# An encoder layer on one core: which engine copies the first up pair's sums, and in what order its second pieces and the LN1 columns run

## The chip, the cores and the metric

The kernel runs on one core of a Trainium2 chip. The metric is the device time of one execution in microseconds (us). TensorE (PE in the profile) does the matrix products, VectorE (DVE), ScalarE (ACT) and GpSimd (POOL) the elementwise work, and SyncE (SP) issues most DMAs. PSUM is the memory that matrix products are written to. Every engine has a queue of its own, and semaphores hold an instruction until what it needs is there.

## The reference, cut to what matters

Two batches, 512 and 256 tokens of 1024 channels, go through one layer with shared weights. `u` is 2 x 2816 wide; the change lies where the first LayerNorm of the layer passes over into the product `x @ w_up`.

```
x = layernorm(x)                                         # ln_in
proj = x @ w_in                                          # 1024 -> 3072
y = concat(rmsnorm(conv mixer), rmsnorm(2-D neighbourhood attention))
x = layernorm(ALPHA * x + y @ w_o, ln1_g, ln1_b)         # LN1
u = dwconv3(x @ w_up, ffn_conv_w, ffn_conv_b)            # 1024 -> 2 * 2816
gate, val = split(u)
x = layernorm(ALPHA * x + (gelu(gate) * val) @ w_down)   # 2816 -> 1024
```

## The kernel before, in words

The 768 tokens are kept as six tiles of 128 (`acc[t]`), tiles 0, 2, 4 of even tokens and 1, 3, 5 of odd ones. All operands are split in a high and a low fp32r part (`split`, lines 98 to 100: ScalarE casts the high part, VectorE or GpSimd subtracts for the low one), and a product is three fp32r products.

**The way into the up projection.** `wo_conv(t)` (lines 815 to 827) ends the mixer's output projection of a tile and normalises it: VectorE adds the product to `acc[t]` (L823), sums up (L824, L209), ScalarE squares (L210), VectorE and GpSimd make the inverse root (L211, L212), VectorE the offset (L826), and ScalarE applies both (L827). `x_tr(t)` (lines 833 to 845) transposes the tile on TensorE (L250) in two halves of four blocks of 128 and applies LN1's gain and offset by column while it takes them out of PSUM: eight instructions a tile, on ScalarE (L844) or, for the second half of odd tiles, on VectorE (L842). `x_even(a)` and `x_odd(a)` (lines 852 to 870) split the columns and make the sums that the products want (L862 to L869), which land in the tile `AR`, seven operands with 386 columns each; columns 0 to 255 come from tiles 0 to 3, columns 257 to 384 from tiles 4 and 5.

**An up pair.** 22 channel blocks of `gate` and of `val` are done pair by pair, c = 0 to 21. A pair takes seven products instead of eight (a Strassen-like scheme for even and odd tokens, gate and value), called by number: `step(c, i)` (lines 951 to 989) with i = 1, 7, 6, 2, 4, 5, 3. One product is 12 matmuls of 386 columns (L180). Four PSUM banks take the sums, called roles 1 to 4: product 1 is written to role 1, which is copied to role 2 (L957); product 7 to role 4, copied to an SBUF tile `M7` (L963); product 6 is added to role 2, which is copied to role 3 (L966); product 2 is added to role 1, product 4 to role 2, products 5 and 3 to role 3. So product 2 may be added to role 1 only once role 1 is copied, and product 4 to role 2 only once that is copied. These copies are ScalarE's before the change. Weights of a product are made by `prep` (a ScalarE cast and a VectorE subtraction of 512 columns), up to three products ahead.

**The first pair.** For c = 0, products 1, 7, 6, 2 and 4 are done in two pieces: columns 0 to 255 as soon as tiles 0 to 3 are there (`a1 a7 a6 a2 a4` in the list of line 999), and columns 256 to 385 in the later loop (the second pieces), as those need tiles 4 and 5. In the list, `w5` is `wo_conv(5)`, `e2` is `x_even(2)` (tile 4) and `o2` is `x_odd(2)` (tile 5).

**What sets the order.** In the stretch of line 999 the order on every engine but SyncE is made by the scheduler of the language, which starts from the order of the code and moves instructions past each other; from line 1125 on TensorE keeps the order of `seq` (line 1007), while the other engines are still ordered by the scheduler. Each engine then works its queue from the front.

Of the kernel before, what the change touches and what calls it, by code (L numbers as in the profile page):

```python
# [48 lines left out]
def encoder_kernel(ctx, tc, x, lnp, wv, wproj, wo_a, wo_c, wup, wdn, chan, rpb, mask, ident, out):  # L49
    nc = tc.nc  # L50
    V, A, G, PE, SP = nc.vector, nc.scalar, nc.gpsimd, nc.tensor, nc.sync
    PS = bass.MemoryType.PSUM

    def pool(name, **kw):
        g = tc.tile_pool(name=name, bufs=1, reuse_waits="tile", **kw)
        p = g.__enter__()
        return p, lambda: g.__exit__(None, None, None)
# [11 lines left out]
    def f(ap):  # L69
        return ap.bitcast(F32)  # L70
# [112 lines left out]
    a1, a1_close = pool("a1", side="right")  # L183
# [62 lines left out]
    def transposed(q, src):  # L246

        q = q.rearrange("p (k n) -> p k n", k=4)
        for k in range(4):
            PE.transpose(q[:, k], src[:, k], idt)  # L250
        return q
# [73 lines left out]
    for z in "w0 w1 w2 w3 w4 w5 x1 w6 x2 w7 x3 c0 x4 x5".split():  # L325
        n = int(z[1])
# [72 lines left out]
    a2, a2_close = pool("a2", side="right")  # L399
# [140 lines left out]
    R, M7, K = {}, {}, {}  # L540
# [208 lines left out]
    def bank(name):  # L749
        return ps.tile([P, 512], F32, name=name, tag="bank", bufs=8)  # L750
# [39 lines left out]
    for n in range(2):  # L790
        order = (4, 5, 0, 1, 2, 3)
        banks = {t: bank("wo") for t in order}
        for kk in range(2):
# [3 lines left out]
            for k in range(2):  # L797
                i = 2 * kk + k
# [13 lines left out]
    def kn(z):  # L812
        return z.rearrange("p (k n) -> p k n", n=P)
# [19 lines left out]
    def x_tr(t):  # L833

        z = []
        for c in range(2):
            q = transposed(bank("tr"), kn(acc[t])[:, 4 * c:4 * c + 4])
            z.append(lp.tile([P, 4, P], F32, name="zt", bufs=7))
            for k in range(4):
                i = 4 * c + k  # L840
                if c and t % 2:
                    V.tensor_scalar(z[c][:, k], q[:, k], g1[:, i:i + 1], b1[:, i:i + 1], op0=OP.mult, op1=OP.add)  # L842
                else:
                    A.activation(z[c][:, k], q[:, k], AF.Identity, bias=b1[:, i:i + 1], scale=g1[:, i:i + 1])  # L844
        return z
# [6 lines left out]
    def x_even(a):  # L852
        xq[a] = x_tr(2 * a)
        for c in range(2):
            x_op(xq[a][c], c, a)

    def x_odd(a):
        el, eh = xq.pop(a)
        ol, oh = x_tr(2 * a + 1)
        x_op(oh, 2, a)  # L860
        es = engs(TE[4 * a:4 * a + 4])
        V.tensor_sub(el, el, ol)  # L862
        x_op(el, 3, a, es[0])
        V.tensor_sub(ol, oh, ol)
        x_op(ol, 5, a, es[1])
        z = lp.tile([P, 4, P], F32, name="zt", bufs=7)
        V.scalar_tensor_tensor(z, el, -1.0, oh, op0=OP.mult, op1=OP.subtract)
        x_op(z, 4, a, es[2])
        V.scalar_tensor_tensor(eh, z, -1.0, eh, op0=OP.mult, op1=OP.subtract)  # L869
        x_op(eh, 6, a, es[3])  # L870
# [18 lines left out]
    def taps_even(c, u, w, b):  # L889

        A.activation(c[:, 0], u, AF.Identity, bias=b, scale=w[:, 1:2])
        A.activation(c[:, 1], u, AF.Identity, bias=b, scale=w[:, 0:1])  # L892
        tap(c, 1, u, 1, w[:, 2:3])

    def taps_odd(c, u, w):
        tap(c, 1, u, 0, w[:, 1:2])
        tap(c, 0, u, 0, w[:, 2:3])
        tap(c, 0, u, -1, w[:, 0:1])

    def cut():  # L900
        return fp.tile([P, 2, HT], F32, name="cu", bufs=6)
# [9 lines left out]
    def gated(c):  # L911

        g, v = ct.pop(c)
        V.tensor_mul(g, g, v)  # L914
        j = c // 2
        if c % 2 == 0:
            h_out(j, 0, 1, g[:, 0:1])
            ho[j] = g
            return
        o = ho.pop(j)  # L920
        h_out(j, 1, 2, g)
        z = fp.tile([P, 3, HT], F32, name="ho", bufs=1)
        V.tensor_sub(z[:, 0], g[:, 1], o[:, 1])
        V.tensor_sub(o[:, 1], o[:, 0], o[:, 1])
        h_out(j, 3, 1, o[:, 1:2])
        V.scalar_tensor_tensor(z[:, 1], o[:, 1], -1.0, g[:, 1], op0=OP.mult, op1=OP.subtract)
        V.scalar_tensor_tensor(z[:, 2], z[:, 1], -1.0, g[:, 0], op0=OP.mult, op1=OP.subtract)
        h_out(j, 4, 3, z)

    pairs, R, M7 = {}, {}, {}  # L930
# [7 lines left out]
    def role(c, i):  # L938
        if (c, i) not in R:
            R[c, i] = bank("u")[:, 0:HT]  # L940
            if i in (2, 3) and c < 2:
                w = pairs[c].w[1 if i == 2 else 6][:, 0]
                PE.matmul(R[c, i], w[:, 0:P], w[:, 0:HT], start=True, stop=True, skip_group_check=True)
        return R[c, i]

    def rest(q, n):

        if n.stop < HT:
            V.memset(q[:, n.stop:HT], 0.0)

    def step(c, i, n=slice(0, HT)):

        k = pairs[c]
        if i == 1:
            k.prod(1, role(c, 1)[:, n], n.start == 0, False, n)
            rest(role(c, 1), n)
            A.copy(role(c, 2)[:, n], role(c, 1)[:, n])  # L957
        elif i == 7:
            k.prod(7, role(c, 4)[:, n], n.start == 0, True, n)
            rest(role(c, 4), n)  # L960
            if c not in M7:
                M7[c] = fp.tile([P, HT], F32, name="m7", bufs=2) if c else M70()
            A.copy(M7[c][:, n], role(c, 4)[:, n])  # L963
        elif i == 6:
            k.prod(6, role(c, 2)[:, n], False, False, n)
            A.copy(role(c, 3)[:, n], role(c, 2)[:, n])  # L966
        elif i == 2:
            k.prod(2, role(c, 1)[:, n], False, True, n)
            if n.stop == HT:
                ct[c] = [cut(), None]  # L970
                taps_even(ct[c][0], role(c, 1), fw[:, c], fb[:, c:c + 1])
        elif i == 4:
            k.prod(4, role(c, 2)[:, n], False, True, n)
            if n.stop == HT:
                k.v = cut()
                V.tensor_add(k.v[:, 0], role(c, 2), M7[c])
        elif i == 5:
            k.prod(5, role(c, 3), False, False)
            v = ct[c][1] = cut()
            V.tensor_add(k.v[:, 1], role(c, 3), M7[c])  # L980
            taps_even(v, k.v[:, 0], fwn[:, c], fb[:, NC + c:NC + c + 1])
            taps_odd(v, k.v[:, 1], fwn[:, c])
        else:
            k.prod(3, role(c, 3), False, True)
            g = ct[c][0]
            taps_odd(g, role(c, 3), fw[:, c])
            A.activation(g, g, AF.Gelu_apprx_tanh)
            gated(c)
            pairs.pop(c)

    def M70():
        return ring.tile([P, 512], F32, name="raw", bufs=NRAW)[:, 0:HT]

    PIECE = {z: n for z in (1, 7, 6, 2, 4) for n in (slice(Z0, HT),)}
    EM = {"w": wo_conv, "e": x_even, "o": x_odd, "l": load_up,
          "p": lambda i: pairs[0].prep(i), "a": lambda i: step(0, i, slice(0, Z0))}
    V.memset(f(AR[:, :, :, :, Z0:Z0 + 1]), 0.0)
    V.memset(f(AR[:, :, :, :, Z1:Z1 + 1]), 0.0)
    for z in "l0 l1 w0 p1 w1 e0 w2 o0 p7 w3 e1 p6 w4 o1 p2 w5 e2 p4 a1 a7 o2 a6 a2 a4 p5".split():
        EM[z[0]](int(z[1]))  # L1000
    lp_close()
    bp_close()
# [3 lines left out]

    seq = []
    for c in range(NC):
        z = [(c, i) for i in (1, 7, 6, 2, 4, 5)]
        if c:  # L1010
            z.insert(2, (c - 1, 3))
        seq += z
    ready = {(0, i) for i in (1, 7, 6, 2, 4, 5)}

    def prepare(c, i):
# [109 lines left out]
    with tc.manual_schedule(engines={PE.engine}):  # L1125
        for n, (c, i) in enumerate(seq):
            if i == 7 and 0 < c < NC - 1:
                load_up(c + 1)
            step(c, i, PIECE[i] if c == 0 and i in PIECE else slice(0, HT))
            for z in seq[n + 1:n + 1 + AHEAD]:  # L1130
                prepare(*z)
            if i == 7:
                sw_slot(len(SEQB) + c)
            if c == NC - 1 and i == 1:
                load(NE)
            if c == NC - 1 and i in (6, 4):
                prep(done[1] + 1)
# [3 lines left out]
        prep(3)  # L1141
        prepare(NC - 1, 3)
        step(NC - 1, 3)
        prep(4)
        fp_close()
# [96 lines left out]
```

## Time and profile before

| | us |
|---|---|
| median of 3 runs | 865.4 |
| the three runs | 865.4, 857.47, 865.75 |
| the profiled execution, own time | 857.87 |
| its span, first to last instruction | 856.1 |

The profile is of one execution; own time and span differ by 1.8 us. In its rows, TensorE is PE, its weight loads PEld; L180 is line 180 of the kernel. A timeline row gives start, duration, engine, line, operation, output<-input, shape, count and, in square brackets, how long the engine was idle before it and what it was waiting for. Equal instructions that follow each other without idle time are one row with a count. The granted clock of TensorE stands in the window rows as PEclk, 1.00 for 2.4 GHz and 0.50 for 1.2 GHz.

### The profile page before, as it was taken

To read this page: it belongs to the slowest core of one execution; us is meant where nothing else is said; L and a number is where in the kernel's file an instruction comes from. 1 tells how busy PE (TensorE), PEld (TensorE's weight loads), DVE (VectorE), ACT (ScalarE), POOL (GpSimd) and SP (SyncE) were. 2 spreads that over 40 slices of the span, in tenths; PEclk is the share of its full clock that TensorE was granted. 3 is DMA by queue.
4 is the path that set the end of the run, shared out by engine and by line. 5 is a ranking of instruction groups with operands and counts; after the bars stand their busy time and mean duration, and the time that the engine had idled before them with its cause. 6 is when DMAs were issued, how large, how long until landed. Compare 5 with 4: busy or idle time off the path is not lost.

```text
span 856.1 us, 13322 instructions
## 1 busy us (share of the span) xinstructions
PE 814.3 (95%) x4391; PEld 750.1 (88%) x4391; DVE 684.7 (80%) x1335; ACT 494.1 (58%) x1020; POOL 231.3 (27%) x286
## 2 busy tenths in 40 slices
PE   4899999999999999899999999999999999999995
PEld 3678998989898777899999999999999968888884
DVE  6997757877876658788889888888989679995675
ACT  4755655665776448765656565555656357565060
POOL 3565361263402521222333243332211000000102
PEclk9999999999999999899999999999999999999998
DMA  8688868866836740496998998899752199894361
GB/s 323 214 211 212 181 178 201 192 174 145 205 105 217 256 105 20 97 239 180 260 239 229 239 258 229 234 250 231 205 162 87 38 326 367 298 289 167 120 235 74
DMA packets 86421, 171.02 MB, mean 200 GB/s; under 512 B 12848, under 2 KB 26400, under 8 KB 86000
## 3 DMA queue, kind: packets, MB, share of 16 engines
q1 hardware_dynamic: 59552, 110.87, 39.7%
q0 software_dynamic: 25216, 54.74, 28.8%
q10 hardware_dynamic: 1584, 4.56, 1.4%
q8 instruction: 34, 0.56, 0.3%
q14 instruction: 35, 0.29, 0.1%
HBM read 142.70 MB, written 50.48 MB: 226 GB/s over the span
## 4 chain that ended last, share of the span: by engine, by line
PE 72%; DVE 10%; DMA 8%; ACT 4%; issue 3%; POOL 2%; SPq 0%; POOLq 0%; ACTq 0%; DVEq 0%
PE u L180 38%; PE dn L1062 17%; PE r L180 9%; DMA raw<-in_wproj 3%; DVE w L100 2%; DMA acc<-xa_d 2%; PE vp L303 2%; DMA br<-in_rpb 1%; PE O L680 1%; PE S L623 1%; PE tr L250 1%; DMA gb<-in_lnp 1%; DVE AR L100 1%; PE PT L656 1%; ACT sq L210 1%
## 5 line engine op out<-in xcount | busy, mean ns | idle before, releaser
L180 PE MATMUL u<-AR,w 128*128 128x386 f32 (+2 forms) x1908 | 333.7, 337 | 3.3 <-ACT u L957 3.3
L180 PEld LDWEIGHTS u<-AR,w 128*128 128x128 f32 x1908 | 332.4, 190 | 3.7 <-ACT u L957 3.5
L100 DVE TENSOR_TENSOR w<-raw,w 128x512 fp32r<-128x512 f32 x248 | 172.8, 708 | 54.4 <-ACT w L99 53.3
L99 ACT CAST w<-raw 128x512 fp32r<-128x512 f32 x255 | 156.5, 619 | 91.6 <-PE r L180 27.5
L1062 PE MATMUL dn<-w,hs 128*128 128x512 f32 (+1 forms) x714 | 164.2, 391 | 2.0 <-DVE hs L100 1.9
L1062 PEld LDWEIGHTS dn<-w,hs 128*128 128x128 f32 x714 | 132.3, 190 | 33.5 <-DVE hs L100 2.4
L180 PE MATMUL r<-AR,w 128*128 128x384 f32 x840 | 158.6, 341 | 2.5 <-ACT w L99 0.7
L180 PEld LDWEIGHTS r<-AR,w 128*128 128x128 f32 x840 | 145.4, 189 | 4.1 <-ACT w L99 1.0
L364 POOL DMA_DIRECT2D sw_d<-in_wdn x44 | 37.2, 918 | 107.9 <-DMA sw_d<-sw_d 86.2
L887 DVE SCALAR_TENSOR_TENSOR cu<-u,ch,cu 128x385 f32<-128x385 f32 (+1 forms) x88 | 52.1, 613 | 11.4 <-ACT cu L892 7.3
L99 ACT CAST hs<-hr 128x386 fp32r<-128x386 f32 x73 | 37.6, 515 | 36.7 <-DMA hr<-h_d 33.5
L100 DVE TENSOR_TENSOR w<-rw,w 128x512 fp32r<-128x512 f32 x70 | 47.0, 685 | 8.4 <-ACT w L99 8.4
L99 ACT CAST w<-rw 128x512 fp32r<-128x512 f32 x70 | 43.4, 623 | 15.4 <-issue 12.0
L887 DVE SCALAR_TENSOR_TENSOR cu<-cu,fwn 128x385 f32<-128x385 f32 (+1 forms) x88 | 48.5, 613 | 0.4 <-ACT cu L892 0.4
L1084 POOL TENSOR_TENSOR mv<-mv,expo 128x1 f32<-128x1 f32 x6 | 7.3, 1219 | 151.3 <-DVE mv L1085 151.3
L909 POOL DMA_DIRECT2D h_d<-cu x33 | 24.1, 731 | 84.8 <-DVE cu L914 80.0
L100 DVE TENSOR_TENSOR hs<-hr,hs 128x386 fp32r<-128x386 f32 x73 | 40.1, 551 | 5.3 <-ACT hs L99 5.2
L801 PE MATMUL wo<-w,AR 128*128 128x512 f32 x144 | 34.2, 395 | 0.7 <-DVE acc L807 0.7
L822 PE MATMUL woc<-w,AR 128*128 128x512 f32 x144 | 34.7, 397 | 0.0
L801 PEld LDWEIGHTS wo<-w,AR 128*128 128x128 f32 x144 | 26.8, 188 | 7.1 <-DVE acc L807 1.2
L822 PEld LDWEIGHTS woc<-w,AR 128*128 128x128 f32 x144 | 26.8, 188 | 6.1
L303 PE MATMUL vp<-w,AR 128*128 128x512 f32 x108 | 29.3, 417 | 2.7 <-DVE AR L100 1.1
(193 smaller groups left out, 1074.9 us busy)
## 6 DMA issues: line engine op xcount, KB each, us to landing
raw<-in_wup SPq DMA_DIRECT2D x60, 256.0 KB, 6.9
hr<-h_d SPq DMA_DIRECT2D x73, 193.0 KB, 4.7
raw<-in_wproj SPq DMA_DIRECT2D x50, 256.0 KB, 5.1
rw<-in_wup SPq DMA_DIRECT2D x50, 256.0 KB, 6.8
sw_d<-in_wdn POOLq DMA_DIRECT2D x44, 256.0 KB, 9.1
raw<-sw_d SPq DMA_DIRECT2D x44, 256.0 KB, 4.7
raw<-in_wdn SPq DMA_DIRECT2D x33, 256.0 KB, 4.8
h_d<-ho POOLq DMA_DIRECT2D x11, 579.0 KB, 3.8
```

What stands on the lines that cost most here:

```text
L99: A.copy(hi, src)
L100: eng.tensor_sub(lo, src, f(hi))
L180: PE.matmul(q, w[:, g, k], AR[:, OPS[i], h, k, n], start=start and m == 0, stop=stop and m == 11, skip_group_check=True)
L210: A.activation(scratch, src, AF.Square, bias=mv[:, 0:1], accum_out=mv[:, 2:3])
L250: PE.transpose(q[:, k], src[:, k], idt)
L303: PE.matmul(q, x_part(t, c)[:, h, k], wvo[4 * c + k][:, g], start=c + m + k == 0, stop=c == 1 and m == 2 and k == 3)
L364: return lambda: G.dma_start(sw_d[j, SW[i]], src, accum_op=OP.add)
L801: PE.matmul(banks[t], yas(h, i, t), wt[k][:, g], start=i == 0 and m == 0, stop=i == 3 and m == 2)
L822: PE.matmul(q, ycs(h, i, t), woc[i][n][:, g], start=i == 0 and m == 0, stop=i == 3 and m == 2)
L887: V.scalar_tensor_tensor(c[:, e, n], u[:, m], w, c[:, e, n], op0=OP.mult, op1=OP.add)
L909: G.dma_start(h_d[j, i:i + n].rearrange("o p n -> p o n"), src)
L1062: PE.matmul(q[:, x], hs[i, j][:, h, cols(a)], wd[i, j][:, g, x], start=i in (1, 7) and j == 0 and m == 0, stop=j == NJ - 1 and m == 2, ski ...
```

## The change

Four edits, all at the first up pair:

1. `x_tr`: the second half of tile 4 takes its columns by VectorE (L842 stands now for tiles 1, 3, 4 and 5), where ScalarE took all eight of tile 4.
2. `step`: for c = 0 the three copies between sums (role 1 to role 2, role 4 to `M7`, role 2 to role 3) are VectorE's, in both pieces; six instructions.
3. The list: `o2` stands behind `a6 a2 a4` instead of ahead of them.
4. `seq`: the second pieces come in the order 1, 2, 7, 6, 4 instead of 1, 7, 6, 2, 4, and the next pair's product 1 (c = 1) is moved in behind the second piece of product 2.

```
@@ x_tr
-                if c and t % 2:
+                if c and t not in (0, 2):
                     V.tensor_scalar(z[c][:, k], q[:, k], g1[:, i:i + 1], b1[:, i:i + 1], op0=OP.mult, op1=OP.add)
                 else:
                     A.activation(z[c][:, k], q[:, k], AF.Identity, bias=b1[:, i:i + 1], scale=g1[:, i:i + 1])
@@ step
+        cp = A.copy if c else V.tensor_copy
         if i == 1:
             k.prod(1, role(c, 1)[:, n], n.start == 0, False, n)
             rest(role(c, 1), n)
-            A.copy(role(c, 2)[:, n], role(c, 1)[:, n])
+            cp(role(c, 2)[:, n], role(c, 1)[:, n])
...
-            A.copy(M7[c][:, n], role(c, 4)[:, n])
+            cp(M7[c][:, n], role(c, 4)[:, n])
...
-            A.copy(role(c, 3)[:, n], role(c, 2)[:, n])
+            cp(role(c, 3)[:, n], role(c, 2)[:, n])
@@ the list
-    for z in "l0 l1 w0 p1 w1 e0 w2 o0 p7 w3 e1 p6 w4 o1 p2 w5 e2 p4 a1 a7 o2 a6 a2 a4 p5".split():
+    for z in "l0 l1 w0 p1 w1 e0 w2 o0 p7 w3 e1 p6 w4 o1 p2 w5 e2 p4 a1 a7 a6 a2 a4 o2 p5".split():
@@ seq
-        z = [(c, i) for i in (1, 7, 6, 2, 4, 5)]
+        z = [(c, i) for i in ((1, 7, 6, 2, 4, 5) if c else (1, 2, 7, 6, 4, 5))]
         if c:
             z.insert(2, (c - 1, 3))
         seq += z
+
+    seq.remove((1, 1))
+    seq.insert(2, (1, 1))
```

TensorE's queue around the first pieces, before. The weights `w_3492` are those of product 7, `w_3557` of product 6, `w_3632` of product 2, `w_3696` of product 4; `tr<-idt,acc_2963` are the transposes of tile 5, and `waits` names the engine whose semaphore holds the row.

```order
L180 MATMUL u<-AR,w_3492 128x256 x10
L180 MATMUL u<-AR,w_3557 128x256 [waits Activation_49]
L180 MATMUL u<-AR,w_3557 128x256 [waits DVE_49]
L180 MATMUL u<-AR,w_3557 128x256 x8
L250 MATMUL tr<-idt,acc_2963 128x128 [waits Activation_49]
L250 MATMUL tr<-idt,acc_2963 128x128 x3
L250 MATMUL tr<-idt,acc_2963 128x128 [waits DVE_49]
L250 MATMUL tr<-idt,acc_2963 128x128 x3
L180 MATMUL u<-AR,w_3557 128x256 x2
L943 MATMUL u<-w_3557 128x386
L180 MATMUL u<-AR,w_3632 128x256 [waits DVE_49]
```

The same place in the changed kernel, in the same queue:

```order
L180 MATMUL u<-AR,w_3492 128x256 x10
L943 MATMUL u<-w_3557 128x386
L250 MATMUL tr<-idt,acc_2963 128x128 [waits Activation_49]
L180 MATMUL u<-AR,w_3557 128x256 [waits DVE_49]
L180 MATMUL u<-AR,w_3557 128x256 x11
L180 MATMUL u<-AR,w_3632 128x256 x12
L180 MATMUL u<-AR,w_3696 128x256 [waits DVE_49]
L180 MATMUL u<-AR,w_3696 128x256 [waits Pool_49]
L180 MATMUL u<-AR,w_3696 128x256 x10
L250 MATMUL tr<-idt,acc_2963 128x128 x7
```

One transpose of tile 5, which waits for ScalarE's L827, stands ahead of product 6 now; the seven others have moved behind product 4. Next, TensorE's second pieces before (`w_3356` is product 1, `w_3882` the next pair's product 1):

```order
L180 MATMUL u<-AR,w_3356 128x130
L180 MATMUL u<-AR,w_3356 128x130 [waits DVE_49]
L180 MATMUL u<-AR,w_3356 128x130 x10
L180 MATMUL u<-AR,w_3492 128x130 [waits Activation_49]
L180 MATMUL u<-AR,w_3492 128x130 [waits DVE_49]
L180 MATMUL u<-AR,w_3492 128x130 x10
L180 MATMUL u<-AR,w_3557 128x130 [waits Activation_49]
L180 MATMUL u<-AR,w_3557 128x130 [waits DVE_49]
L180 MATMUL u<-AR,w_3557 128x130 x10
L180 MATMUL u<-AR,w_3632 128x130 x12
```

In the changed kernel (`w_3838` is the next pair's product 1):

```order
L180 MATMUL u<-AR,w_3356 128x130 x12
L180 MATMUL u<-AR,w_3632 128x130 [waits DVE_49]
L180 MATMUL u<-AR,w_3632 128x130 x11
L180 MATMUL u<-AR,w_3838 128x386 [waits Activation_49]
L180 MATMUL u<-AR,w_3838 128x386
L180 MATMUL u<-AR,w_3838 128x386 [waits DVE_49]
L180 MATMUL u<-AR,w_3838 128x386 x9
L943 MATMUL u<-w_3838 128x386
L180 MATMUL u<-AR,w_3492 128x130 [waits Activation_49]
L180 MATMUL u<-AR,w_3492 128x130 x11
```

Product 2 stands right behind product 1 now, and its first matmul has a wait for VectorE. Last, VectorE's queue of the changed kernel from the first copy on (L958, L964 and L967 are the three copies, L957, L963 and L966 before):

```order
L826 TENSOR_TENSOR mv<-mv 128x1 [waits Pool_49]
L949 MEMSET u 128x130 [waits PE_49]
L100 TENSOR_TENSOR AR<-zt,AR 128x4x128 [waits Activation_49]
L958 COPY u<-u 128x256 [waits DVE_49]
L964 COPY raw<-u 128x256 [waits DVE_49]
L967 COPY u<-u 128x256 [waits PE_49]
L842 TENSOR_SCALAR zt<-tr,ch 128x128 [waits PE_49]
L842 TENSOR_SCALAR zt<-tr,ch 128x128 x3
L862 TENSOR_TENSOR zt<-zt 128x512 [waits Activation_49]
L864 TENSOR_TENSOR zt<-zt 128x512 [waits DVE_49]
L100 TENSOR_TENSOR AR<-zt,AR 128x4x128 [waits Activation_49] x3
L867 SCALAR_TENSOR_TENSOR zt<-zt 128x512
L958 COPY u<-u 128x130 [waits PE_49]
```

The copy of product 1's second piece (the last row) stands behind the four L842 of tile 5 and behind six more instructions of `x_odd(2)`; the copies of 256 columns stand behind the offset of tile 5's LayerNorm (L826).

## Rows read from the trace of the kernel before

**Rows 1.** The page: the chain that ended last, by engine.
```profile
PE 72%; DVE 10%; DMA 8%; ACT 4%; issue 3%; POOL 2%; SPq 0%; POOLq 0%; ACTq 0%; DVEq 0%
```

**Rows 2.** TensorE's waits over the whole span: total us, times, longest.
```profile
PE u L180 <- ACT u L957: 3.3, 1, 3.3
...
PE dn L1062 <- DVE hs L100: 1.9, 1, 1.9
```

**Rows 3.** Windows by stage: length, busy us (count) by engine, PEclk, DMA.
```profile
core 0: us, PE busy (x) PEld busy (x) DVE busy (x) ACT busy (x) POOL busy (x), PEclk, DMA share, GB/s
...
344.78:348.05 3.27, 0.01 (x2) 0.01 (x1) 1.73 (x6) 3.21 (x8) 1.15 (x3) 0.87 0.14 55
348.05:354.05 6.00, 6.00 (x27) 6.00 (x28) 2.52 (x7) 3.72 (x8) 2.72 (x4) 0.50 0.74 114
354.05:356.23 2.18, 2.18 (x20) 2.18 (x19) 2.15 (x5) 1.49 (x3) 0.00 (x0) 1.00 0.27 48
356.23:363.07 6.84, 6.84 (x63) 6.72 (x61) 5.80 (x9) 4.57 (x11) 0.00 (x0) 1.00 0.07 16
363.07:392.30 29.23, 29.23 (x167) 29.23 (x167) 24.37 (x41) 18.02 (x32) 7.55 (x10) 1.00 0.86 220
392.30:680.00 287.70, 287.70 (x1625) 287.24 (x1625) 252.12 (x432) 167.97 (x294) 77.96 (x99) 1.00 0.76 208
```

**Rows 4.** Timeline of TensorE, 334 to 352 us.
```profile
334.22 1.09 PE L250 MATMUL tr<-idt,acc 128*128 128x128 f32 x8 [1.12 <-ACT acc L827]
335.07 5.82 PE L822 MATMUL woc<-w,AR 128*128 128x512 f32 x24
...
343.20 1.58 PE L180 MATMUL u<-AR,w 128*128 128x256 f32 x12
...
348.05 2.50 PE L180 MATMUL u<-AR,w 128*128 128x256 f32 x10 [3.26 <-ACT u L957]
350.35 1.91 PE L250 MATMUL tr<-idt,acc 128*128 128x128 f32 x8
```

**Rows 5.** Timeline of ScalarE, same stretch.
```profile
345.94 1.18 ACT L210 ACTIVATE sq<-acc,mv 128x1024 f32<-128x1024 f32 x1
...
347.59 0.40 ACT L957 COPY u<-u 128x256 f32<-128x256 f32 x1
348.37 1.24 ACT L827 ACTIVATE acc<-acc,mv 128x1024 f32<-128x1024 f32 x1 [0.38 <-DVE mv L826]
```

**Rows 6.** Timeline of VectorE, same stretch and on to 357 us.
```profile
343.95 0.74 DVE L823 SCALAR_TENSOR_TENSOR acc<-woc,ra,acc 128x512 f32<-128x512 f32 x1
...
344.80 0.64 DVE L824 TENSOR_TENSOR mv<-mv 128x1 f32<-128x1 f32 x1
...
345.55 0.14 DVE L209 TENSOR_SCALAR mv<-mv 128x1 f32<-128x1 f32 x1
...
352.29 1.36 DVE L842 TENSOR_SCALAR zt<-tr,ch 128x128 f32<-128x128 f32 x4 [3.42 <-PE tr L250]
...
356.71 0.68 DVE L867 SCALAR_TENSOR_TENSOR zt<-zt 128x512 f32<-128x512 f32 x1
```

**Rows 7.** Groups by line and shape, ScalarE and VectorE, 340 to 372 us: mean ns.
```profile
L844 ACT ACTIVATE zt<-tr,ch 128x128 f32<-128x128 f32 x12 | 4.6, 460 | 1.6 <-PE tr L250 1.6
...
L957 ACT COPY u<-u 128x130 f32<-128x130 f32 x1 | 0.3, 258 | 0.0
...
L100 DVE TENSOR_TENSOR w<-raw,w 128x512 fp32r<-128x512 f32 x7 | 4.6, 686 | 0.0
...
L842 DVE TENSOR_SCALAR zt<-tr,ch 128x128 f32<-128x128 f32 x4 | 1.4, 404 | 3.4 <-PE tr L250 3.4
...
L976 DVE TENSOR_TENSOR cu<-u,raw 128x386 f32<-128x386 f32 x1 | 0.6, 552 | 0.0
```

**Rows 8.** Windows behind TensorE's other wait, near 690 us, as in rows 3.
```profile
692.00:694.00 2.00, 2.00 (x6) 1.38 (x5) 2.00 (x5) 1.44 (x3) 0.00 (x0) 0.50 1.01 387
694.00:696.00 2.00, 2.00 (x7) 1.57 (x7) 0.81 (x2) 0.52 (x1) 0.00 (x0) 0.65 1.07 390
```

## The prediction

> **What bounds the kernel now.** I read the page's chain first: TensorE makes up 72% of it [rows 1]. The reader should see that a gain or loss counts only where TensorE stands still or runs slowly. Next came the list of TensorE's waits. In the up projection it has one, 3.3 us for ScalarE's copy L957, and at the passage to the down projection one of 1.9 us [rows 2]. The windows by stage show what surrounds the first [rows 3]. From 344.78 to 348.05 us TensorE does nothing and ScalarE is busy for 3.21 of 3.27 us. Then come 6.00 us at a granted clock of 0.50 (1.2 GHz), and from 354.05 on full clock. From there to 680 us TensorE is busy without a break (29.23 of 29.23, 287.70 of 287.70), so what is lost or won here reaches the end one for one.
>
> The wait itself costs 3.3 us and the low clock about half of 6.0 us, so some 6 us lie here. Two timelines say why: ScalarE takes its square L210 at 345.94 and L827 at 348.37, with the copy between them at 347.59 [rows 5], and TensorE starts product 6 at 348.05 [rows 4].
>
> **First hold: the transpose ahead of product 6.** In the changed queue one transpose of tile 5 stands ahead of product 6, and it needs L827's result. That TensorE does not pass a waiting transpose is in the trace: at 334.22 it was idle for 1.12 us for L827 of another tile, and 24 matmuls of L822 that stand behind the transposes started only at 335.07 [rows 4]. So moving the copy to VectorE no longer frees product 6; L827 of tile 5 does.
>
> When does it end? Before, it ended at 348.37 + 1.24 = 349.61. ScalarE loses four column instructions (460 ns, L844) and the copies [rows 7], but the square still needs VectorE's L209, and behind L823 (to 344.69) stand now L842, L824, L842, L209. One L842 costs 404 ns [rows 7], and four in a row took 1.36 [rows 6], 0.32 apart. L824 took 0.64 right behind L823 [rows 6]; apart from it, it may take 0.1. L209 is then done between 345.5 and 346.2, against 345.69 before. From the square's start to L827's end it took 349.61 - 345.94 = 3.67, so L827 ends between 349.2 and 349.9; I take 349.3, since L842 gives L823 time to finish. TensorE, done with product 7 and the moved-up seed at about 344.95, stands for 4.35 us, 1.1 longer than before.
>
> Behind it lie the same 36 matmuls and 8 transposes that ran from 348.05 to 356.23. Low clock took 6.00 / 27 = 0.222 us each, full clock 2.18 / 20 = 0.109 [rows 3]. If the clock returns at 354.05 again, 21 are done by then and 23 take 2.5: 356.55, **0.3 later**. If it stays low for 6.0 us from the restart, 27 are done at 355.3 and 17 take 1.9: 357.2, **1.0 later**. I take 0.6.
>
> **Second hold: product 2's second piece.** Seven transposes of tile 5 have moved behind product 4. VectorE's `x_odd(2)` hangs on them: in the trace it starts at 352.29, as the transposes end (350.35 + 1.91 = 352.26), and L867 ends at 356.71 + 0.68 = 357.39, 5.1 us after the transposes [rows 4, 6]. The copy of product 1's second piece comes behind L867 in VectorE's queue, and product 2, next on TensorE, may not start without it. Only product 1's second piece covers this: 12 matmuls at 6.84 / 60 = 0.114, 1.4 us [rows 3]. The hold is 5.1 + the copy - 1.4.
>
> The trace has no VectorE copy out of PSUM. ScalarE's of 130 columns took 258 ns; VectorE's nearest, 128 columns out of PSUM, 404 ns; the 386 column sum took 552 [rows 7]. The copy lies between 0.25 and 0.55; I take 0.4, the row nearest in engine and length. The hold is 4.1 us (4.0 to 4.3). Before, ScalarE copied aside of this chain and TensorE did not stop (6.84 of 6.84). [...]
>
> **The clock behind the second hold.** 3.26 us of idleness brought a stretch at 1.2 GHz of which 6.0 us lay under TensorE's work [rows 3, 4]. Near 690 us 1.9 us of idleness brought a shorter one: 0.50 in 692 to 694 and 0.65 in 694 to 696 [rows 2, 8], about 3.4 us low. A low us with TensorE at work costs half: 3.0 or 1.7. With 4.1 us idle I expect the longer kind and take 2.7; no fall would be 0.
>
> **Third hold: product 4's second piece** waits for the copy role 2 to role 3, which in VectorE's queue follows `M7`'s copy, a weight subtraction (w_3943) and L173. That subtraction needs a cast whose buffer product 7's second piece frees. From that piece's end: cast 0.62, subtraction and L173 two slots of 0.6 to 0.69, copy 0.3 to 0.4, about 2.4 us; product 6's second piece covers 1.4. I take 1.1 (0 to 1.5).
>
> **What costs nothing.** The seeds and the next pair's product 1 are moved, not added. Product 1's low weights are subtracted two places behind that L958 copy, 1.4 to 2 us later; product 2's piece (1.4 us, or 2.7 at 1.2 GHz) hides that, and if the clock is full up to 0.6 us is bare. The four L842 and six copies on VectorE (3.3 us) lie where it was busy 1.73 of 3.27 us [rows 3], or are counted above. ScalarE's freed time ends no wait. GpSimd's and SyncE's queues keep their order; loads of later pairs wait some us longer for buffers that are wanted three pairs of about 15 us later.
>
> **Sum:** 0.6 + 4.1 + 2.7 + 1.1 = **8.5 us slower**, 5.4 if the clock does not fall a second time (and product 4's wait with it shrinks to 0.7), up to 13 with all upper ends (1.0 + 4.3 + 1.5, 3.4 if TensorE works through all of a low stretch of 6.8 us, and a third stretch of up to 3). On the profiled execution's own time that is 857.9 + 8.5 = 866.4. The shown runs form two groups 8 us apart: 857.47 and the profiled 857.87, and 865.4 and 865.75. Nothing in the one profile tells what parts them or which a median will fall in. I count from the middle of the groups, 861.6: **870.1 us**. The upper group gives 874.1, the lower 866.1.
>
> **Rivals.**
>
> *The clock falls more often* (15%): the three holds come within 25 us, and 1.9 us of idleness was enough once [rows 2, 8], so the third can extend the low stretch. For it speaks that row, against it that the eight transposes behind the 1.12 us wait at 334 us took 1.09 us, where eight at 1.2 GHz took 1.91 [rows 4]. 12 us slower: 873.6.
>
> *No second fall* (10%): the second hold costs only itself: +5.4, 867.0. Against it speak both waits that the trace shows, each followed by 0.50.
>
> *Not slower, by the groups* (13%): the upper group might be executions in which ScalarE's wait at 345 us leaves the clock low for longer. The changed kernel has that wait no more, and if its holds are all of the cheap kind, every run lies near 857.6 + 5.4 = 863.0, under the old median. It decides if the runs of the changed kernel lie in one group. Against it: 8 us is 16 us of low clock, and the trace shows 6.
>
> *The change does what it says* would mean that TensorE passes the transposed tile's wait and goes on with product 6 when VectorE's copy is there. That copy stands behind L826 and a subtraction, so it ends near 349.0 anyway; this is worth 0.3 us and no case of its own.
>
> **How the numbers follow.** The forecast has 62%, the three rivals 15, 10 and 13. About 1% is what a measurement of this kernel can tell from no change, 856.7 to 874.1. Of the forecast's 62, 37 fall within 1% (the lower group, and half of the upper, which lies on the bound) and 25 above. The first rival adds 6 within and 9 above, the second 10 within, the last 9 within and 4 below: slower 34, same 62, faster 4. The range is 860 to 878: from the last rival's group less 3, to the upper group with +12.5.
>
> **What would show it.** Right: TensorE idle for over 4 us with L827 (`acc`) as its releaser and L250 as the row behind it; a second wait of about 4 us with VectorE's L958 as releaser; two stretches at 0.50 instead of one before 380 us; a third wait of about 1 us behind L967. Wrong: product 6's first piece starting before L827 ends, no wait between the second pieces of products 1 and 2, or a wait there that ends on ScalarE.

## The result and the profile after

The changed kernel takes 870.2 us (median of 20 runs, 866.45 to 876.59), the kernel before 862.0 us (20 runs, 857.45 to 867.66). The ratio is 1.0101, 95% interval [1.008, 1.0122]: slower by about 1%. Each ratio in this document comes from the single runs, without those more than 1.5% above the fastest of their kernel (two of the twelve with 15 extra matmuls, 876.59 and 880.46 us), and is not the quotient of the medians. The profiled execution took 868.32 us, its span is 866.5 us.

First the list of TensorE's waits (us in total, times, longest). The one wait for L957 [rows 2] is gone. In its place stand a wait of 4.6 us for L827, as the longest of its row, and two for the copies L958 and L967, which VectorE makes now.

```profile
PE tr L250 <- ACT acc L827: 7.0, 4, 4.6
PE u L180 <- DVE u L958: 4.1, 1, 4.1
...
PE u L180 <- DVE u L967: 1.1, 1, 1.1
```

TensorE's timeline of the changed kernel shows the three holds and the work between them; its columns are those of [rows 4].

```profile
344.81 1.58 PE L180 MATMUL u<-AR,w 128*128 128x256 f32 x12
346.23 0.34 PE L943 MATMUL u<-w 128*128 128x386 f32 x1
351.18 0.33 PE L250 MATMUL tr<-idt,acc 128*128 128x128 f32 x1 [4.61 <-ACT acc L827]
351.26 6.04 PE L180 MATMUL u<-AR,w 128*128 128x256 f32 x36
357.14 0.93 PE L250 MATMUL tr<-idt,acc 128*128 128x128 f32 x7
357.82 1.53 PE L180 MATMUL u<-AR,w 128*128 128x130 f32 x12
363.47 6.06 PE L180 MATMUL u<-AR,w 128*128 128x130 f32 x24 [4.11 <-DVE u L958]
...
369.55 2.79 PE L180 MATMUL u<-AR,w 128*128 128x130 f32 x24
373.47 11.60 PE L180 MATMUL u<-AR,w 128*128 128x130 f32 x60 [1.13 <-DVE u L967]
```

One transpose, 0.33 us long, holds product 6 until ScalarE's L827 is done; product 2's second piece stands for 4.11 us behind the copy of product 1's, product 4's for 1.13. VectorE's timeline says why the second hold is that long:

```profile
346.22 0.41 DVE L842 TENSOR_SCALAR zt<-tr,ch 128x128 f32<-128x128 f32 x1
346.55 0.51 DVE L824 TENSOR_TENSOR mv<-mv 128x1 f32<-128x1 f32 x1
346.99 0.40 DVE L842 TENSOR_SCALAR zt<-tr,ch 128x128 f32<-128x128 f32 x1
347.31 0.14 DVE L209 TENSOR_SCALAR mv<-mv 128x1 f32<-128x1 f32 x1
347.37 0.71 DVE L842 TENSOR_SCALAR zt<-tr,ch 128x128 f32<-128x128 f32 x2
...
350.48 0.42 DVE L958 COPY u<-u 128x256 f32<-128x256 f32 x1
...
358.11 1.37 DVE L842 TENSOR_SCALAR zt<-tr,ch 128x128 f32<-128x128 f32 x4 [3.64 <-PE tr L250]
...
362.52 0.68 DVE L867 SCALAR_TENSOR_TENSOR zt<-zt 128x512 f32<-128x512 f32 x1
363.12 0.29 DVE L958 COPY u<-u 128x130 f32<-128x130 f32 x1
```

The last row is the copy that product 2 waits for. It stands behind `x_odd(2)`, from 358.11 on, and that begins only as the transposes end (357.14 + 0.93 = 358.07). The first copy, at 350.48, is late as well: behind L823 VectorE does tile 4's four L842 now, and the copy stands behind L826, at 349.63.

The windows by stage, columns as in [rows 3], show the clock (1.00 is the full clock, 0.50 half of it):

```profile
346.56:351.18 4.62, 0.01 (x2) 0.01 (x2) 3.97 (x14) 2.99 (x4) 2.62 (x5) 1.00 0.06 23
351.18:357.14 5.96, 5.96 (x37) 5.96 (x38) 0.47 (x2) 0.00 (x0) 1.11 (x2) 0.71 0.81 132
...
359.36:363.47 4.11, 0.00 (x0) 0.00 (x0) 4.08 (x9) 2.49 (x5) 0.00 (x0) 0.79 0.00 0
363.47:369.37 5.90, 5.90 (x25) 5.90 (x25) 4.17 (x7) 2.76 (x5) 0.00 (x0) 0.57 0.01 3
...
373.47:385.25 11.78, 11.78 (x62) 11.78 (x63) 8.56 (x15) 4.15 (x7) 2.40 (x4) 0.86 0.82 220
385.25:425.40 40.15, 40.15 (x228) 40.15 (x228) 34.49 (x59) 25.26 (x43) 12.04 (x16) 1.00 0.78 203
```

In this trace the clock is either 1.00 or 0.50, so a row's low time is (1 - PEclk) / 0.5 of its length. TensorE at work loses a little less than half of it: here a matmul of 386 columns starts 0.321 us behind the one before at 0.50, which is 1.2 columns a ns, and 0.177 at 1.00, one of 130 columns 0.213 and 0.111 (medians). Counted as half, that is 5.96 x 0.29 = 1.7 us behind the first hold, 5.90 x 0.43 = 2.5 behind the second, 11.78 x 0.14 = 1.6 behind the third. From 385.25 to 690 us TensorE is busy without a break at full clock (304.75 of 304.75 us, PEclk 1.00), as before.

To compare kernels I count one stretch in each timeline: from the start of the first 256-column piece until 288 matmuls of 386 columns are done. It takes 72.89 us before and 82.27 after, 9.4 more; this is one execution of each, while the medians differ by 8.2. Two parts of it are worth telling apart. The first part, from product 7's first piece to product 1's second piece, takes 13.03 us before and 13.01 after; the second part, from there to the end of the stretch, 58.2 us before and 67.6 after. In these two executions the whole loss lies in the second part.

### The profile page after: what moved, and what is told of

Read it like the earlier page. It is cut to its first block, busy times and chain, and to the rows that moved or that the text cites. A ratio compares the mean times of both kernels' runs of the same rounds, so it can differ in the third digit from the quotient of the medians.

```text
span 866.5 us, 13323 instructions
## 1 busy us (share of the span) xinstructions
PE 818.1 (94%) x4391; PEld 753.1 (87%) x4391; DVE 690.3 (80%) x1345; ACT 491.2 (57%) x1010; POOL 228.3 (26%) x286
## 3 DMA queue, kind: packets, MB, share of 16 engines
q10 hardware_dynamic: 1584, 4.56, 1.4%
## 4 chain that ended last, share of the span: by engine, by line
PE 76%; DVE 10%; DMA 6%; ACT 3%; issue 3%; POOL 1%; SPq 0%; POOLq 0%; DVEq 0%; ACTq 0%
PE u L180 38%; PE dn L1066 18%; PE r L180 13%; DVE w L100 2%; PE vp L303 2%; DMA acc<-xa_d 2%; DMA raw<-in_wproj 2%; PE O L680 1%; DVE AR L100 1%; PE S L623 1%; PE tr L250 1%; PE PT L656 1%; DMA gb<-in_lnp 1%; ACT acc L827 1%; ACT sq L210 1%
## 5 line engine op out<-in xcount | busy, mean ns | idle before, releaser
L180 PE MATMUL u<-AR,w 128*128 128x386 f32 (+2 forms) x1908 | 337.2, 339 | 5.2 <-DVE u L958 4.1
L180 PEld LDWEIGHTS u<-AR,w 128*128 128x128 f32 x1908 | 335.8, 192 | 5.6 <-DVE u L958 4.3
L100 DVE TENSOR_TENSOR w<-raw,w 128x512 fp32r<-128x512 f32 x248 | 174.9, 716 | 56.7 <-ACT w L99 55.7
L99 ACT CAST w<-raw 128x512 fp32r<-128x512 f32 x255 | 156.6, 619 | 99.1 <-PE r L180 27.4
L99 ACT CAST hs<-hr 128x386 fp32r<-128x386 f32 x73 | 37.5, 514 | 34.5 <-DMA hr<-h_d 32.7
L99 ACT CAST w<-rw 128x512 fp32r<-128x512 f32 x70 | 43.5, 624 | 15.3 <-issue 11.7
L1088 POOL TENSOR_TENSOR mv<-mv,expo 128x1 f32<-128x1 f32 x6 | 4.4, 728 | 153.4 <-DVE mv L1089 153.4
```

Of the source, the lines that this page charges most:

```text
L99: A.copy(hi, src)
L100: eng.tensor_sub(lo, src, f(hi))
L180: PE.matmul(q, w[:, g, k], AR[:, OPS[i], h, k, n], start=start and m == 0, stop=stop and m == 11, skip_group_check=True)
```

## The experiments

Theory: the loss is three holds and the low clock behind them, and comes from two parts of the change. VectorE's column work for tile 4 lets the scheduler move a waiting transpose ahead of product 6, and VectorE's copies of the second pieces stand behind `x_odd(2)`. Rivals: the new order of the second pieces costs by itself, and the clock alone makes the loss. Line numbers are those of the changed kernel.

**The four edits undone one at a time.** Edit 1:

```
-                if c and t not in (0, 2):
+                if c and t % 2:
```

> The change without its first edit: the second half of tile 4's LN1 columns is ScalarE's again. The scheduler then leaves tile 5's transposes behind product 4, and VectorE's first copy right behind L209. Theory (three holds plus their clock): TensorE's first wait shrinks from 4.6 us to about 1 us, for VectorE's copy, and no low clock follows it (1.7 us); the second wait, 4.1 us for L958, and the third of 1.1 us stay. 4.5 to 6 us faster than the changed kernel, about 865. Rival (the columns on VectorE are a help, since they free ScalarE for 1.5 us): 870 or up to 1.5 us slower, first wait unchanged.

865.33 us (10 runs, 862.72 to 871.24), ratio to before 1.0035 [1.0001, 1.0069]; the stretch takes 76.17 us. TensorE's timeline, at the place of the first two holds:

```profile
348.15 4.52 PE L180 MATMUL u<-AR,w 128*128 128x256 f32 x36 [1.18 <-ACT AR L99]
352.50 1.03 PE L250 MATMUL tr<-idt,acc 128*128 128x128 f32 x8
353.29 1.53 PE L180 MATMUL u<-AR,w 128*128 128x130 f32 x12
358.94 6.40 PE L180 MATMUL u<-AR,w 128*128 128x130 f32 x24 [4.11 <-DVE u L958]
```

No transpose stands ahead of product 6, the eight lie behind product 4, and product 6 waits 1.18 us instead of 4.61. On VectorE the copy follows L209 at once:

```profile
347.53 0.14 DVE L209 TENSOR_SCALAR mv<-mv 128x1 f32<-128x1 f32 x1
347.55 0.45 DVE L958 COPY u<-u 128x256 f32<-128x256 f32 x1
```

The copy is done at 348.00, and the last thing that product 6 waits for, by the trace, is ScalarE's cast L99, done at 348.07. The first part takes 353.29 - 345.21 = 8.08 us, 4.9 less than before the change and after it. The total came out as the theory said: 0.66 points of the 1.01 per cent, the larger part, go with edit 1, in the company of the others. With it gone VectorE's copies do what they say: they let product 6 start early. The second hold is unchanged.

Of edit 2 the copies of the second pieces go back to ScalarE:

```
-        cp = A.copy if c else V.tensor_copy
+        cp = V.tensor_copy if not c and n.start == 0 else A.copy
```

> The change with the copies of the second pieces (three of 130 columns) on ScalarE again; the copies of 256 columns stay on VectorE. Theory (the copy's place in VectorE's queue behind the chain of x_odd(2) makes the second hold): the first wait stays at 4.6 us, the second falls from 4.1 to under 2 us (ScalarE's copy stands behind two casts only), the third under 0.6, and the low clock behind the second becomes shorter. 3 to 5 us faster than the changed kernel, about 866. Rival (the transposes behind product 4 hold TensorE whichever engine copies, through the operands that x_odd(2) makes): the same wait of 4 us at another line, 870.

869.35 us (10 runs), ratio 1.006 [1.0027, 1.0093]; stretch 78.37 us.

```profile
361.45 6.50 PE L180 MATMUL u<-AR,w 128*128 128x130 f32 x24 [1.58 <-ACT u L958]
...
371.57 10.11 PE L180 MATMUL u<-AR,w 128*128 128x130 f32 x60 [0.34 <-ACT u L967]
```

The first hold stays (4.58 us), the second falls from 4.11 to 1.58 and the third from 1.13 to 0.34, as the theory said, but the clock still goes down in the profiled execution (0.54 in the 6.62 us from 361.45). The second part takes 63.7 us, 3.9 less than in the changed kernel and 5.5 more than before. The theory's total, 866, was missed, the rival's 870 is nearer; as the intervals of this kernel and of the changed one overlap, that the total falls is likely, not shown.

Edit 3, the list:

```
-    for z in "l0 l1 w0 p1 w1 e0 w2 o0 p7 w3 e1 p6 w4 o1 p2 w5 e2 p4 a1 a7 a6 a2 a4 o2 p5".split():
+    for z in "l0 l1 w0 p1 w1 e0 w2 o0 p7 w3 e1 p6 w4 o1 p2 w5 e2 p4 a1 a7 o2 a6 a2 a4 p5".split():
```

> The change with o2 in its old place in the list, ahead of a6 a2 a4. All eight transposes of tile 5 then stand ahead of product 6. Theory: the first wait stays (4.6 us for L827), the second shrinks to about 2 us since the chain of x_odd(2) starts some 5 us earlier, the third stays at about 1 us. 2 to 3.5 us faster than the changed kernel, about 867.5. Rival (the list's order alone makes the loss): back to the kernel before, 862.

868.34 us (10 runs), ratio 1.0078 [1.0045, 1.0111]; stretch 78.08. Holds of 4.74, 1.20 and 1.03 us: `x_odd(2)` runs earlier and the second hold is short, the first stays. The second part takes 62.2 us, 5.4 less than in the changed kernel, and the first 1.2 more. The intervals of this one and of the changed kernel overlap; that the total falls is likely, not shown.

Edit 4, the order of the second pieces, is put back to 1, 7, 6, 2, 4, and the two lines that move the next pair's product 1 are taken out:

```
-        z = [(c, i) for i in ((1, 7, 6, 2, 4, 5) if c else (1, 2, 7, 6, 4, 5))]
+        z = [(c, i) for i in (1, 7, 6, 2, 4, 5)]
...
-    seq.remove((1, 1))
-    seq.insert(2, (1, 1))
```

> The change with the old order of the second pieces and of the next pair's first product. Behind product 1's second piece stands product 7, which doesn't need product 1's copy, but an operand of x_odd(2) that is ready some 3.5 us after the transposes. Theory: first wait 4.6 us as in the changed kernel, second about 2.5 to 3.5 us with another releaser (a cast or subtraction into AR), third gone; 2 to 4 us faster than the changed kernel, about 867. Rival (the order of the second pieces costs nothing as the work is the same): 870, with a wait of 4 us.

870.87 us (5 runs), ratio 1.0093 [1.0053, 1.0134]; stretch 83.58, the longest of all. The waits did fall, to 2.46 and 0.51 us, and the third is gone. But look at the clock in its windows, the second holds the waits:

```profile
360.22:363.53 3.31, 0.34 (x3) 0.19 (x2) 3.27 (x7) 2.26 (x4) 0.00 (x0) 1.00 0.00 0
363.53:377.20 13.67, 13.67 (x58) 13.67 (x59) 8.56 (x16) 6.16 (x10) 0.87 (x1) 0.50 0.28 70
377.20:385.00 7.80, 7.80 (x45) 7.80 (x45) 5.86 (x11) 3.25 (x6) 1.65 (x2) 1.00 0.66 184
```

Behind 3 us of waiting TensorE ran for 13.67 us at 0.50 though busy all the time: counted as half, 6.8 us lost, 2.7 more than behind the last two holds of the changed kernel, where the shorter waits gave back 2.3. The total is the rival's 870, not the theory's 867. So undoing the order alone brought nothing in these five runs. Whether the order costs something by itself they can't tell, as the clock covers it.

**Both parts undone, and edit 1 alone.** The next two start from the two ends: the changed kernel without edit 1 and without the second-piece copies (both lines as above),

> The change without its first edit and with the second pieces' copies on ScalarE: of the change stay VectorE's copies of the first pieces, the list and the order of the second pieces. Theory: first wait about 1.2 us without low clock, second about 1.6 us, third under 0.4; the stretch from the first piece of 256 columns to the products of the third pair takes 71 to 73.5 us (72.9 before, 82.3 changed), so 860 to 863, the loss is gone and the gain is no more than 2 us. Rival (each edit carries a cost of its own that adds up): 866.

861.77 us (10 runs), ratio 1.0002 [0.9972, 1.0032]; stretch 72.98 against 72.89 before. With the two undone the loss is gone, within 0.3%. But what remains, edits 3 and 4 and VectorE's copies of the first pieces, is not free; it gains and loses about the same:

```profile
354.87 1.53 PE L180 MATMUL u<-AR,w 128*128 128x130 f32 x12
358.00 1.96 PE L180 MATMUL u<-AR,w 128*128 128x130 f32 x14 [1.59 <-ACT u L958]
360.92 3.45 PE L180 MATMUL u<-AR,w 128*128 128x386 f32 x10 [0.95 <-DVE w L100]
...
367.61 10.11 PE L180 MATMUL u<-AR,w 128*128 128x130 f32 x60 [0.45 <-ACT u L967]
```

The first part takes 354.87 - 346.76 = 8.11 us, 4.9 less than before, as VectorE's copies let product 6 start early. The second part takes 63.2 us, 5.0 more than before, with three waits that the kernel before does not have there (1.59, 0.95 and 0.45 us) and a clock of 0.54 in the 3.45 us from 360.92. The first wait is product 2's, right behind product 1, the second the next pair's product 1, for its weights: both stand where edit 4 put them. So the rival that the order costs by itself still stands. No run undoes edit 3 or edit 4 in this kernel, so which of them costs how much, and whether VectorE's first copies alone would beat the kernel before, is not shown. And the kernel before with edit 1 only:

```
-                if c and t % 2:
+                if c and t not in (0, 2):
```

> The kernel before with the first edit alone (tile 4's second half by VectorE). TensorE's queue keeps the order of the kernel before. Theory: ScalarE's first copy comes some 0.3 us earlier, since VectorE's L842 now stand before L209; the wait is 2.9 to 3.2 us instead of 3.26, the low clock stays: same as before within 0.5 us (862). Rival (the columns are the harmful edit by themselves, through L209 and L827): 3 to 4 us slower.

859.65 us (10 runs), ratio 0.998 [0.9953, 1.0007]; stretch 71.27. So the costliest edit is harmless by itself: with ScalarE's copies and the list of before, the scheduler leaves the transposes where they were, and the hold is the old one for the copy. The wait, 3.17 us, is the forecast's; the low clock that the theory left behind it did not come (see the last section).

```profile
352.21 1.45 PE L180 MATMUL u<-AR,w 128*128 128x256 f32 x10 [3.17 <-ACT u L958]
353.79 1.09 PE L250 MATMUL tr<-idt,acc 128*128 128x128 f32 x8
```

**Is the low clock a cost of its own?** The second hold of the changed kernel is filled: 22 matmuls of 386 columns into a bank in which their results are overwritten, unused, ahead of product 2's second piece. What is computed is the same.

```
         elif i == 2:
+            if not c and n.start:
+                w = k.w[6][:, 0]
+                for _ in range(22):
+                    PE.matmul(role(1, 1), w[:, 0:P], w[:, 0:HT], start=True, stop=True, skip_group_check=True)
             k.prod(2, role(c, 1)[:, n], False, True, n)
```

> The change with 22 extra matmuls of 386 columns between the second pieces of products 1 and 2, where TensorE stands for 4.1 us; they write a bank that the next pair's product 1 starts over. They take 3.9 us at full clock and change nothing that is computed. Theory (a part of the loss is the low clock that the second hold brings): the hold shrinks to some 0.3 us, product 2's second piece starts no earlier, the 6.8 us of low clock behind it and perhaps the third stretch are gone, and from the first piece of 256 columns to the products of the third pair it takes 2 to 4 us less than in the changed kernel (82.3 us); about 867.5 in all. Rival (the waits alone make the loss, the clock is a symptom): the same 82 us and 870, or more by what of the filling sticks out.

> The same kernel as f1_fill_second_hold, with more runs, because its four runs lay 6 us apart. Theory (2.5 to 2.7 us of the change's loss is the low clock behind the second hold): 867.5 to 868.5. Rival (filling the hold changes nothing of the total, since the clock falls somewhere else instead): 870 to 872.

The first time 873.85 us (4 runs, 870.54 to 876.91), ratio 1.0131 [1.0081, 1.018]; the second time, on another chip, 868.99 us (8 runs, 865.41 to 871.5), ratio 1.0082 [1.0049, 1.0115]. Timeline and windows of the second:

```profile
361.43 4.10 PE L972 MATMUL u<-w 128*128 128x386 f32 x22
365.71 3.82 PE L180 MATMUL u<-AR,w 128*128 128x130 f32 x24 [0.18 <-DVE u L958]
```

```profile
361.43:365.71 4.28, 4.10 (x25) 3.78 (x24) 4.25 (x9) 2.50 (x5) 0.00 (x0) 1.00 0.00 0
365.71:372.34 6.63, 6.63 (x49) 6.33 (x49) 5.63 (x10) 4.38 (x8) 0.00 (x0) 1.00 0.13 42
...
373.46:385.12 11.66, 11.66 (x62) 11.66 (x62) 8.40 (x15) 4.16 (x7) 2.03 (x3) 0.85 0.72 197
```

The 24 matmuls behind the hold (12 of product 2's piece and 12 of 386 columns of the next pair; a row names the first shape) took 6.06 us in the changed kernel and take 3.82 here, at full clock. From product 1's second piece to the stretch's end it is 65.40 us here and 67.58 in the changed kernel: 2.2 us are the clock's, as a cost apart from the wait. The profile of the first series agrees, with 3.83 and 65.35 us. The low stretch behind the third hold stays (0.85). The totals don't show the gain: the first series lies above the changed kernel, the second 1.2 us below, and both intervals overlap its interval; 868.99 is between the theory's 867.5 to 868.5 and the rival's 870 to 872. In the first series' profiled execution (876.91 us, one of the two long ones) part of the time went elsewhere: in the attention stage TensorE waits 3.12 us at 147 us and 3.61 us, for a load, at 195 us, and behind both waits most of its matmuls of L623 take 0.41 us each. The changed kernel's profile has a wait of 1.09 us at the first place and none for that load, and at both places most of these matmuls take 0.28 us.

The same for the long low stretch of the kernel with edit 4 undone: 15 such matmuls ahead of product 7's second piece.

```
         elif i == 7:
+            if not c and n.start:
+                w = k.w[6][:, 0]
+                for _ in range(15):
+                    PE.matmul(role(1, 1), w[:, 0:P], w[:, 0:HT], start=True, stop=True, skip_group_check=True)
             k.prod(7, role(c, 4)[:, n], n.start == 0, True, n)
```

> The changed kernel with the order of the second pieces put back, as in u4_seq_back, and 15 idle products of 386 columns (results unused, nothing else changed) put ahead of product 7's second piece, where u4_seq_back waited 2.46 and 0.51 us and then ran 13.65 us at half the clock. Theory (the low clock behind the wait is most of that kernel's loss): the waits of 2.46 and 0.51 us are filled, the low stretch behind 363 us is gone, which gives back about 6.8 us, and the stretch from the first 256-column piece to the 288th 386-column matmul takes 76 to 79 us (83.6 in u4_seq_back); total 864 to 867. Rival (the clock falls whatever fills the hold, or the waits themselves are the loss): the stretch stays at 82 us or more and the total at 870 to 872.

869.74 us (12 runs, 862.64 to 880.46), ratio 1.0084 [1.0051, 1.0117]: next to the rival's number, the theory missed. The execution that was profiled is its longest, so its stretch of 82.41 us says little about the median. In this execution the fill did not keep the clock up; whether it did in the others is not shown. The hold is filled, two waits of 0.50 and 0.42 us remain, and behind them the clock is low again:

```profile
375.50:378.04 2.54, 1.62 (x14) 1.45 (x13) 2.54 (x6) 1.25 (x3) 0.00 (x0) 1.00 0.03 6
378.04:390.00 11.96, 11.96 (x54) 11.96 (x55) 7.60 (x15) 5.42 (x9) 0.87 (x1) 0.57 0.35 88
```

What sets when the clock falls behind waits of half a microsecond stays open.

**A version that beats both.** Keep edits 1 and 4, leave all copies to ScalarE, put `o2` back, and start product 1's first piece ahead of tile 4's columns, so that its copy is asked for before ScalarE's LN1 work of tile 5:

```
-        cp = A.copy if c else V.tensor_copy
+        cp = A.copy
...
-    for z in "l0 l1 w0 p1 w1 e0 w2 o0 p7 w3 e1 p6 w4 o1 p2 w5 e2 p4 a1 a7 a6 a2 a4 o2 p5".split():
+    for z in "l0 l1 w0 p1 w1 e0 w2 o0 p7 w3 e1 p6 w4 o1 p2 w5 a1 e2 p4 a7 o2 a6 a2 a4 p5".split():
```

> An attempt at a faster kernel: all copies on ScalarE, the first edit and the order of the second pieces of the change, and product 1's first piece (a1) called right behind wo_conv(5), ahead of tile 4's columns, so that its copy stands ahead of tile 5's square and columns in ScalarE's queue. Theory: no wait above 1 us between 340 and 380 us and no low clock there; the stretch takes 70 to 71.5 us instead of 72.9, 860 (858.5 to 861.5). Rival (the scheduler's other orders cost as much as the wait did): 862 to 864.

856.45 us (12 runs, 854.5 to 862.94) against 860.39 before on the same chip, ratio 0.9945 [0.9916, 0.9975], a little faster than the forecast's range. Its timeline and clock:

```profile
348.70 3.52 PE L180 MATMUL u<-AR,w 128*128 128x256 f32 x28 [0.52 <-ACT u L958]
353.22 1.09 PE L250 MATMUL tr<-idt,acc 128*128 128x128 f32 x8 [0.99 <-ACT acc L827]
```

```profile
330.00:360.00 30.00, 26.30 (x168) 22.82 (x166) 24.28 (x61) 25.09 (x50) 6.71 (x8) 1.00 0.29 71
360.00:400.00 40.00, 39.55 (x235) 39.41 (x236) 34.75 (x60) 25.55 (x46) 9.52 (x12) 1.00 0.73 193
```

The one hold of 3.3 us has become six waits with work between them, 0.52 and 0.99 us and behind these 0.64, 0.36, 0.17 and 0.34. They add up to 3.0 us, hardly less than the old hold; what is gone is the low clock, 6.0 us at 0.50 before, as the clock stays at 1.00 here. The stretch takes 71.65 us, 1.2 less than before, though eight transposes (0.8 us) lie within its bounds here that lie ahead of them before: 2.0 us in this execution, where the medians say 3.9. The early start, the place of `o2`, edit 1 and edit 4 come together here; which of them the gain needs was not tested.

## Why the prediction was right

It forecast 870.1 us and slower by 8.5; it is 870.2, by 8.2. That the totals meet within 0.1 us is luck: the base was taken 0.4 too low and the loss 0.3 too high, and in the profile a term that was put at nothing (1.6) outweighs two that came out smaller (0.8 together). The mechanism, three holds at the forecast places with the forecast releasers, is not luck. The terms, as the profiled execution has them:

| term | forecast, us | measured, us | from |
|---|---|---|---|
| first hold, net of the old one | 0.6 | 0.0 | product 7's first piece to product 1's second: 357.82 - 344.81 = 13.01; before 356.23 - 343.20 = 13.03 [rows 3, 4] |
| second hold | 4.1 | 4.1 | the wait for L958 |
| clock behind it | 2.7 | 2.5 | window 363.47 to 369.37 |
| third hold | 1.1 | 1.1 | the wait for L967 |
| third stretch of low clock | 0 | 1.6 | window 373.47 to 385.25 |
| sum | 8.5 | 9.3 | stretch: 9.4 |

*First hold.* Place, releaser and row behind it are as predicted; it was idle for 4.61 us where 4.35 was forecast. The term was mis-sized, because the clock behind it was low for less than before (0.71 against 0.50 in about 6 us, [rows 3]). In the kernel with edit 4 undone, which has the same hold, the same distance is 358.69 - 344.70 = 13.99, a loss of 1.0; over all six profiles with this hold and this queue it lies between 12.95 and 14.04. So -0.1 to 1.0 is what this term does, by execution, against the one profile of before, and the forecast's 0.6 lies within. The old hold varies too: in the kernel with edit 1 alone, with a hold of 3.17 us and no low clock behind it, the distance is 10.54.

*Second and third hold.* Right in size and cause. The copy of 130 columns was taken at 0.4 us and took 0.29 (the row at 363.12); that 0.1 us is made up by the cover, 1.3 us (358.07 to 359.36) where 1.4 was taken. The 256-column copies took 0.42 and 0.41. So for 130 columns ScalarE's copy, 258 ns, was nearer than L842 with its 404 ns for 128 columns [rows 7], the row that I chose as nearest in engine and length.

*Clock.* A stretch of the longer kind behind the second hold was right. That the third hold, 1.1 us, would not be followed by one was wrong: this is the rival "the clock falls more often", in part. Its argument against, that a 1.12 us wait near 334 us left the clock alone, holds for that place and not for this one. It adds 1.6 us in the profile. It does not come each time: without edit 1, behind the same wait (1.12 us), the same 60 matmuls took 10.08 us and not 11.60. That the medians differ by 8.2 and the profiles by 9.4 fits this, but how many of the runs have the third stretch is not shown.

*The two groups.* This step was wrong. It read 857.5, 857.9, 865.4 and 865.8 as two groups 8 us apart. Twenty runs of before lie from 857.45 to 867.66 with no gap above 2 us. The middle of the supposed groups, 861.6, was still near the median of 862.0, so the base came out right by luck, and the rival "not slower, by the groups" has nothing to stand on.

*The change does what it says* was given no case of its own, since VectorE's copy would be late anyway, worth 0.3 us. For the kernel as it stands that is right (copy done at 350.90, L827 at 351.12). But both the lateness and the transpose come with edit 1, in the company of the other edits (by itself it does not move the transposes ahead): without it the copy starts at 347.55 and product 6 waits 1.18 us. The prediction priced the two together and did not say that one edit spoils the other, nor that 4.9 us were to be had in the first part.

## What to carry to other kernels

A copy that frees an accumulator belongs on the engine whose queue has no long dependent chain ahead of it at that time (here product 2's second piece waited 4.11 us for VectorE's copy and 1.58 for ScalarE's); read the queue's order, not the engine's busy share. Where a scheduler makes the order, an edit's price depends on the edits beside it (edit 1: nothing alone, most of the loss in company), so undo parts in pairs as well as singly. A time equal to the old one doesn't mean that what is left costs nothing; compare the parts of the stretch, where a gain of 4.9 us and a loss of 5.0 can hide behind it. A few runs of a kernel with a 10 us spread are no groups: take the middle, and put the spread into the range.

## What the runs showed that was not expected

How the clock answers a wait varies more than its length explains. A wait of 3.26 us was followed by 6.0 us at 0.50 [rows 3]; in the kernel with edit 1 alone a wait of 3.17 us at the same place was followed by none:

```profile
349.04:352.21 3.17, 0.00 (x2) 0.00 (x1) 2.57 (x9) 2.06 (x4) 1.17 (x3) 1.00 0.13 51
352.21:361.00 8.79, 8.58 (x69) 8.18 (x69) 6.91 (x15) 5.96 (x12) 2.69 (x3) 1.00 0.54 89
```

Waits of about half a microsecond to 1.1 us were followed by a fall in some executions (1.13 us in the changed kernel: 0.86 in the 11.78 us behind it; 0.42 us with 15 extra matmuls: 0.57 in 11.96) and not in others (1.12 us without edit 1, 0.52 us in the version that beats both: 1.00 behind them), and once, behind 2.46 and 0.51 us, the low clock lasted 13.67 us under full work. It differs between two executions of one kernel too: the kernel with 22 extra matmuls was profiled twice, with a hold for L827 of 4.57 and of 4.56 us, and the 36 matmuls behind it took

```profile
359.58 7.07 PE L180 MATMUL u<-AR,w 128*128 128x256 f32 x36
```

in the first series and

```profile
353.51 6.03 PE L180 MATMUL u<-AR,w 128*128 128x256 f32 x36
```

in the second. Over a kernel's runs the mean granted clock goes with the time: of the changed kernel's, those at 0.986 and 0.987 took 866 to 870 us, those at 0.978 to 0.980 870 to 877. Where each run lost its clock can't be read without a profile of each, and was not tried.
